# Nine places of a weight pool laid 4128 bytes apart in place of 4096, with a scratch tile of half the size

## The chip, the core and the metric

The kernel runs on one core of a Trainium2 chip. A core has a matrix engine (TensorE, PE in the profile; its loads of the stationary operand are listed apart as PEld), VectorE (DVE), ScalarE (ACT), GpSimd (POOL) and SyncE (SP, which here only issues DMAs). On-chip memory (SBUF) has 128 partitions; a place in it is a byte offset that holds for every partition alike. Matmuls read both operands from SBUF and add into PSUM. The metric is the device time of one execution in microseconds, as the median of several runs.

## The reference, cut to what matters

Two layers, each a token mixer and a SwiGLU channel mixer over 1024 positions and 1024 channels, everything in float32:

```python
D_MODEL, SEQ, DEPTH, D_FF = 1024, 1024, 2, 2816

def hybrid_mixer(h, w_in, ...):
    z = h @ w_in                                  # 1024 x 1536
    y_f = fourier_mix(z[..., :256])               # 2-D DFT over positions and 64 channels
    y_s = spatial_gating(z[..., 256:768], ...)    # gelu, layernorm, 128 x 128 position mixing
    y_a = gqa_attention(z[..., 768:1280], ...)    # 8 q heads, 2 kv heads, rotary positions
    y = jnp.concatenate([rmsnorm(y_f, ...), rmsnorm(y_s, ...), rmsnorm(y_a, ...)], axis=-1)
    return y @ w_out

def swiglu(h, w_gate, w_up, w_down):
    return (jax.nn.silu(h @ w_gate) * (h @ w_up)) @ w_down

for l in range(DEPTH):
    x = x + rmsnorm(hybrid_mixer(rmsnorm(x, g_pre_mix[l]), ...), g_post_mix[l])
    x = x + rmsnorm(swiglu(rmsnorm(x, g_pre_ffn[l]), ...), g_post_ffn[l])
```

## The kernel before

A layer goes through five stages on TensorE: the input projection (tiles `z`, `project`), attention with the DFT and the gating between its steps (`sc`, `ptr`, `pv`), the output projection (`m`, `out_steps`), the gate and up product of the channel mixer (`fx`, `fy`, `ff_prod`), and the down product (`fX`, `fY`, `d_prod`). The last two are done by a seven-product block scheme, so that DVE and POOL form sums and differences of blocks around the matmuls.

Nearly all matmuls stream 512 columns past a stationary block of 128 x 128. Float32 accuracy is had by splitting each operand into a rounded part and a remainder, both of a type called float32r (`split` and `gain_split`: ACT writes the first, DVE or POOL the second). `matmul3` (line 142) runs three matmuls for each pair: first by first, first by remainder, remainder by first. Each matmul brings its own stationary block, so TensorE loads one 128 x 128 block for each matmul, while the matmul before still streams.

The split weights live in a pool `Wp` of nine places. A tile of it holds both parts, 1024 words or 4096 bytes in each partition; the places are used in turn. In it stand the split weights of the input projection (`z_split`, line 297), nine of the sixteen of the output projection (`wo_load`, line 682), those of the gate and up product (`wsplit`, line 132, called by `ff_prep`), and half of the split operands of the down product (`d_prep`). A few others use a place for a while: an identity `id0`, a scratch row `sink`, `gpostf`, and in the last layer four rows `xin` (`ffn_open`). The order of use is that of the code; a tile waits until the readers of the tile before it at its place are done.

The other operands lie elsewhere: `nat` (all activations), the constants and `identr` (the identity of the transposes) stand before `Wp`; the raw weights `rawp` (four places of 4096 bytes), `kT`, `vv`, `hB` and others behind it, on the left side of SBUF; `hT`, `pT`, `yT`, `yFT` and others are laid from the right end down. As built, every operand of a 512-column matmul starts at 256 bytes past a multiple of 512: the large tiles on the left and those on the right all have sizes that are multiples of 512 bytes. So in 8479 of 8487 cases a streamed operand and the block that is loaded for the matmul after it start at the same offset within 512 bytes.

`junk` (line 312) is a scratch tile in which ACT leaves squares that nobody reads; only their sum is used (`sumsq`, line 152). It is 512 elements of bf16, or 1024 bytes, and stands in front of `nat` and of `Wp`.

Of the kernel before, what the change touches and what calls it, by code (L numbers as in the profile page):

```python
# [11 lines left out]
F32 = mybir.dt.float32  # L12
R32 = mybir.dt.float32r
BF16 = mybir.dt.bfloat16
# [4 lines left out]
P = 128  # L19
D = 1024  # L20
# [61 lines left out]
def encoder_kernel(ctx, tc, A, out):  # L82
# [3 lines left out]
    def pool(name, bufs=1, side="left", stack=None):  # L86
        return (stack or ctx).enter_context(tc.tile_pool(name=name, bufs=bufs, side=side, reuse_waits="tile"))

    cst = pool("cst")
    st = pool("st", 6)  # L90

    pool("edge", 1, "right").tile([P, 56], F32, name="edge")
    nat = pool("natp").tile([P, NT, D], F32, name="nat")
    Wp = pool("Wp", 9)
    rawp = pool("rawp", 4)
    psp = ctx.enter_context(tc.tile_pool(name="psp", bufs=1, space=PSUM))
# [18 lines left out]
    asp = dram.tile([DFF, S], F32, name="asp")  # L115


    def split(hi, lo, src, eng=nc.vector):
        nc.scalar.copy(hi, src)  # L119
        eng.tensor_tensor(out=lo, in0=src, in1=hi.bitcast(F32), op=ALU.subtract)  # L120

    def gain_split(w, raw, g):

        nc.scalar.activation(w[:, 0], raw, AF.Copy, scale=g)
        nc.vector.scalar_tensor_tensor(out=w[:, 1], in0=raw, scalar=g, in1=w[:, 0].bitcast(F32), op0=ALU.mult, op1=ALU.subtract)

    def fetch(src, shape, name, p=None):
        raw = (p or rawp).tile([P] + shape, F32, tag="raw", name=f"raw_{name}")
        nc.sync.dma_start(raw, src)
        return raw  # L130

    def wsplit(src, shape, name, p=None, **kw):

        w = (p or Wp).tile([P, 2] + shape, R32, tag="w", name=f"w_{name}", **kw)
        split(w[:, 0], w[:, 1], src)
        return w

    def rows2(w, r0, c0, n):

        return w[r0:r0 + 256, c0:c0 + n].rearrange("(k p) n -> p k n", p=P)  # L140
# [24 lines left out]
    def gain_row(p, src, name, **kw):  # L165
        g = p.tile([P, src.shape[-1]], F32, name=name, **kw)
        nc.sync.dma_start(g, src.partition_broadcast(P))
        return g
# [120 lines left out]
    def z_fetch(l, c, kk):  # L289
        raw = rawp.tile([P, 2, 512], F32, tag="raw", name=f"raw_z{l}_{c}_{kk}")  # L290
        o = 0
        for c0, n in CHUNK[c]:
            nc.sync.dma_start(raw[:, :, o:o + n], rows2(A["w_in"][l], kk * 256, c0, n))
            o += n
        zraw[l, c, kk] = raw

    def z_split(l, c, k):

        w = Wp.tile([P, 2, 512], R32, tag="w", name=f"w_z{l}_{c}_{k}")
        gain_split(w, zraw[l, c, k // 2][:, k % 2], gz[l][:, k:k + 1])  # L300
        zw[l, c, k] = w

# [6 lines left out]
    one, mean = scal[:, 0:1], scal[:, 1:2]  # L309
    nc.gpsimd.memset(one, 1.0)  # L310
    nc.gpsimd.memset(mean, 1.0 / 256)
    junk = cst.tile([P, 512], BF16, name="junk")
    nc.scalar.activation(junk[:, 0:8], mhalf, AF.Square)
    gz_load(0)
    z_fetch(0, 0, 0)
    id0 = Wp.tile([P, P], F32, tag="w", name="id0")
    make_identity(nc, id0)
    identr = cst.tile([P, P], R32, name="identr")
    nc.vector.tensor_copy(identr, id0)
# [6 lines left out]
        x0(t)  # L326
    rope = cst.tile([P, NT, 2, HD], F32, name="rope")
    nc.sync.dma_start(rope, A["c_rope"])
    sink = Wp.tile([P, D], F32, tag="w", name="sink")


    rz = {}
# [23 lines left out]
    for l in range(DEPTH):  # L356
# [26 lines left out]
        for i, g in enumerate(("g_q", "g_k")):  # L383
            nc.sync.dma_start(gqk[:, i, 0, :], A[g][l].partition_broadcast(P))
            a = gqk[:, i, 0, :].rearrange("p (h s f) -> p h s f", h=2, s=2)
# [296 lines left out]
        def wo_load(i):  # L682

            oc, k = i // 8, KORD[i % 8]
            if k % 2 == 0:
                wraw[oc, k // 2] = fetch(rows2(A["w_out"][l], k * P, oc * 512, 512), [2, 512], f"wo{l}_{oc}_{k}", wr if i < 10 else (y2 if i == 14 else rawp))
            raw, g = wraw[oc, k // 2][:, k % 2], gmx[:, k:k + 1]
            w = (Wp if i < 9 else (Yr if i < 11 else W2)).tile([P, 2, 512], R32, tag="w", name=f"w_wo{l}_{oc}_{k}")
            if i < 10:
                nc.gpsimd.tensor_tensor(out=raw, in0=raw, in1=g.to_broadcast([P, 512]), op=ALU.mult)  # L690
                nc.scalar.copy(w[:, 0], raw)
                nc.gpsimd.tensor_tensor(out=w[:, 1], in0=raw, in1=w[:, 0].bitcast(F32), op=ALU.subtract)
            else:
                gain_split(w, raw, g)
            wo[oc, k] = w
# [101 lines left out]
        Yr = pool(f"Yr{l}", 2, "right", sY)  # L797
# [11 lines left out]
        for n, G in enumerate(groups):  # L809
            nxt = groups[n + 1] if n + 1 < len(groups) else None  # L810
            t, g = G
# [56 lines left out]
        W2 = pool(f"W2{l}", 5, "left", sL)  # L868
        yp = pool(f"yp{l}", 1, "right", sY)
        y2 = pool(f"y2{l}", 1, "right", sR)  # L870
        gpost = gain_row(yp, A["g_post_mix"][l], f"gpost{l}")
# [157 lines left out]
        def d_unit(kind, i, shape, dt, name):  # L1029
            p = du[kind]  # L1030
            return p.tile([P] + shape, dt, tag=f"{kind}{i}", name=name, bufs=1)
# [22 lines left out]
        def d_blk(gi, pi, side, b):  # L1054

            r, c = divmod(b, 10)
            j, h = (c, r) if side == 0 else (r, c)
            return draw[gi, pi, side, j - 1][:, (h - 1) * 512:h * 512]

        def d_sums(gi, v):  # L1060
            for pi in range(len(DGROUPS[gi])):
                a = lambda b: d_blk(gi, pi, 0, b)
                w = lambda b: d_blk(gi, pi, 1, b)
                tt = lambda o, x, y, op=ALU.subtract: nc.gpsimd.tensor_tensor(out=o, in0=x, in1=y, op=op)  # L1064
                if v == 5:
                    tt(a(11), a(11), a(21))
                    tt(a(21), a(21), a(22), ALU.add)
                    tt(w(11), w(12), w(11))
                    tt(w(12), w(22), w(12))
                elif v == 6:  # L1070
                    tt(a(21), a(22), a(11))
                    tt(w(11), w(22), w(11))
                elif v == 3:
                    tt(a(12), a(12), a(21))
                elif v == 4:
                    tt(w(21), w(21), w(11))
# [3 lines left out]
        def d_op_slot(s, n):  # L1080

            gi, v = STEPS[s]
            if len(DGROUPS[gi]) == 3:
                return ("W", "W", "W", "W", "W", "W", "W", "W", "W", ("dO", 0), ("dO", 1), ("dO", 2),
                        ("dO", 3), ("dN", 0), ("dN", 1), ("dN", 2), ("dN", 3), ("dN", 4))[s % 3 * 6 + n]
            return {1: "W", 2: "W", 5: ("dO", n), 6: ("dN", n), 3: ("dR", 4 + n), 7: ("dR", n), 4: ("dN", n)}[v]

        def d_prep(s):
            if s >= len(STEPS):
                return  # L1090
            gi, v = STEPS[s]
            d_sums(gi, v)
            n = 0
            for pi in range(len(DGROUPS[gi])):
                for side in range(2):
                    slot = d_op_slot(s, n)
                    nm = f"dw{l}_{s}_{n}"
                    if slot == "W":
                        t = Wp.tile([P, 2, 512], R32, tag="w", name=nm)
                    else:  # L1100
                        t = d_unit(slot[0], slot[1], [2, 512], R32, nm)
                    split(t[:, 0], t[:, 1], d_blk(gi, pi, side, DOPER[v][side]), nc.gpsimd if gi + 1 == len(DGROUPS) and v in (3, 4) and pi else nc.vector)
                    dop[s, pi, side] = t
                    n += 1
# [76 lines left out]
        for n in range(NPROD):  # L1181
            p, j = divmod(n, 14)
# [31 lines left out]
        fin = {}  # L1214

        def ffn_open(t):
            own = last and t > 3
            xin = (Wp if own else rawp).tile([P, D], F32, tag="w" if own else "raw", name=f"xin{l}_{t}")
            fin[t] = Residual(t, t // 4, fin["gpost"], xs, out if last else xs, xin, None, f"po{l}_{t}")

        def fstep(spec):
# [30 lines left out]
        for s, (gi, v) in enumerate(STEPS):  # L1252
            end = gi + 1 == len(DGROUPS)
            for u in range(4):
                if not (end and v == 4):
                    d_tile(s, u)
                if end and v == 7:
                    d_tile(s + 1, u)
            k = DORD.index(v)
            if not end and k < 4:  # L1260
                for n in range(k * 3, min(k * 3 + 3, 4 * len(DGROUPS[gi + 1]))):
                    d_load(gi + 1, n)
            d_prep(s + 3)
            if end and v == 1:
                if not last:
                    rz_tile(l + 1)
                fin["gpost"] = Wp.tile([P, D], F32, tag="w", name=f"gpostf{l}")
                nc.sync.dma_start(fin["gpost"], A["g_post_ffn"][l].partition_broadcast(P))
                if not last:
                    gz_load(l + 1)  # L1270
                    for kk in range(4):
                        z_fetch(l + 1, 0, kk)
            if end and not last:
                if v in (2, 5):
                    for kk in range(4):
                        z_split(l + 1, 0, kk + (4 if v == 5 else 0))
# [34 lines left out]
```

## Time and profile before

| | us |
|---|---|
| median of 3 runs | 2283.14 (2282.67 to 2284.38) |
| the profiled execution | 2282.25 |
| its span, first to last instruction | 2280.5 |
| TensorE busy in the span | 2191.5 |
| VectorE busy | 1607.3 |
| ScalarE busy | 1138.5 |
| GpSimd busy | 952.2 |
| mean granted TensorE clock | 0.983 |

The profile is one execution, taken by the hardware. Its rows name the source line, the engine, the operation and the tiles (written from read), the number of such instructions, and their busy time. The end of a matmul is modelled, so how close matmuls follow one another is read from the start times in the timeline or from the length of a row of many; the duration of a single one is not its cost. Between the span and the execution's own time lie 1.75 us.

### The profile page before, as it was taken

What the parts mean: (1) busy time and instruction counts of PE and PEld (TensorE: products, weight loads), DVE (VectorE), ACT (ScalarE), POOL (GpSimd) and SP (SyncE); (2) the same over time, 40 slices, a digit from 0 to 9 for tenths busy, and PEclk for the clock granted to TensorE, in tenths of its full rate; (3) what the DMA queues carried; (4) which work ended last, traced back from release to release, by engine and by line L of the source; (5) the groups of instructions that cost most, each with busy time, mean ns of one, the idle gap of its engine ahead of it and who ended that gap; (6) DMA issues with size and microseconds to landing.
All of it is one profiled execution on the core that took longest, in us unless ns stands there. A gap on an engine that the chain in (4) does not pass through costs nothing. (4 is left out here: it accounts for less than half of the span.)

```text
span 2280.5 us, 29159 instructions
## 1 busy us (share of the span) xinstructions
PE 2191.5 (96%) x10460; PEld 1807.2 (79%) x10460; DVE 1607.3 (70%) x2457; ACT 1138.5 (50%) x2188; POOL 952.2 (42%) x797
## 2 busy tenths in 40 slices
PE   9999999999999999999899999999999999999986
PEld 7787888878888888877677788888788888877874
DVE  6868986585444447899977698965854444488998
ACT  6338996553333334434452489855533333344333
POOL 2643443243323235655637235332432323266556
PEclk9999999999999999999999999999999999999998
DMA  4110003213132316221331000042132323253212
GB/s 159 42 45 20 19 10 115 99 65 106 61 105 62 104 62 240 111 84 47 107 111 38 17 19 20 10 138 85 61 102 74 93 74 93 74 226 111 83 47 111
DMA packets 104961, 185.28 MB, mean 81 GB/s; under 512 B 12272, under 2 KB 62704, under 8 KB 104816
## 3 DMA queue, kind: packets, MB, share of 16 engines
q1 hardware_dynamic: 103376, 178.70, 23.1%
q0 software_dynamic: 1440, 4.72, 0.7%
q8 instruction: 82, 1.34, 0.2%
q14 instruction: 63, 0.52, 0.1%
HBM read 143.54 MB, written 39.85 MB: 80 GB/s over the span
## 5 line engine op out<-in xcount | busy, mean ns | idle before, releaser
L144 PE MATMUL fx<-hT,w_f 128*128 128x512 f32 x1584 | 374.9, 393 | 6.6 <-ACT nat L1006 4.5
L144 PEld LDWEIGHTS fx<-hT,w_f 128*128 128x128 f32 x1584 | 300.1, 190 | 71.2 <-ACT nat L1006 6.0
L120 DVE TENSOR_TENSOR w_f<-raw_f,w_f 128x512 fp32r<-128x512 f32 x264 | 213.9, 814 | 192.6 <-ACT w_f L119 189.5
L120 DVE TENSOR_TENSOR dw<-dr,dw 128x512 fp32r<-128x512 f32 x300 | 325.4, 1129 | 30.2 <-ACT dw L119 29.9
L144 PE MATMUL z<-w_z,hT 128*128 128x512 f32 x1152 | 286.3, 403 | 11.8 <-DVE rz L196 5.1
L119 ACT CAST dw<-dr 128x512 fp32r<-128x512 f32 x308 | 171.8, 618 | 234.5 <-POOL dr L1064 94.1
L119 ACT CAST w_f<-raw_f 128x512 fp32r<-128x512 f32 x264 | 162.2, 621 | 236.3 <-PE fy L144 196.7
L144 PEld LDWEIGHTS z<-w_z,hT 128*128 128x128 f32 x1152 | 216.6, 193 | 58.6 <-DVE rz L196 5.5
L144 PE MATMUL fX<-dw,dw 128*128 128x512 f32 x1056 | 248.5, 391 | 8.8 <-DVE nat L1123 8.5
L943 POOL TENSOR_TENSOR s<-raw_f,raw_f 128x512 f32<-128x512 f32 x44 | 58.9, 1338 | 459.5 <-DMA raw_f<-in_w_gate_dram 442.1
L144 PE MATMUL fy<-hB,w_f 128*128 128x512 f32 x1056 | 248.0, 390 | 1.9 <-DVE hB L120 1.9
L144 PEld LDWEIGHTS fX<-dw,dw 128*128 128x128 f32 x1056 | 197.1, 188 | 54.8 <-DVE nat L1123 13.9
L144 PEld LDWEIGHTS fy<-hB,w_f 128*128 128x128 f32 x1056 | 198.0, 188 | 43.6 <-DVE hB L120 2.7
L1064 POOL TENSOR_TENSOR dr<-dr,dr 128x512 f32<-128x512 f32 x132 | 220.0, 1696 | 8.6 <-DVE dw L120 8.6
L144 PE MATMUL fY<-dw,dw 128*128 128x512 f32 x792 | 198.3, 408 | 24.1 <-DVE nat L1123 19.3
L997 DVE TENSOR_TENSOR nat<-fy,nat 128x512 f32<-128x512 f32 x132 | 90.9, 690 | 172.3 <-PE fy L144 88.2
L144 PEld LDWEIGHTS fY<-dw,dw 128*128 128x128 f32 x792 | 156.3, 199 | 61.8 <-DVE nat L1123 21.0
L120 DVE TENSOR_TENSOR pT<-ptr,pT 128x512 fp32r<-128x512 f32 x256 | 171.8, 685 | 35.9 <-ACT pT L119 33.5
L752 PE MATMUL pv<-pT,vv 128*128 128x512 f32 x512 | 181.0, 434 | 0.3 <-DVE pT L120 0.3
L119 ACT CAST pT<-ptr 128x512 fp32r<-128x512 f32 x256 | 150.6, 595 | 40.4 <-PE ptr L740 38.1
L1006 ACT COPY nat<-fx 128x512 f32<-128x512 f32 x132 | 77.6, 588 | 183.4 <-PE fx L144 177.7
L723 DVE TENSOR_REDUCE mx<-sc 128x1 f32<-128x1024 f32 x128 | 155.9, 1220 | 10.9 <-PE sc L720 8.9
(208 smaller groups left out, 3746.5 us busy)
## 6 DMA issues: line engine op xcount, KB each, us to landing
raw_f<-in_w_gate_dram SPq DMA_DIRECT2D x44, 512.0 KB, 3.6
raw_f<-in_w_up_dram SPq DMA_DIRECT2D x44, 512.0 KB, 4.1
asp<-nat SPq DMA_DIRECT2D x88, 256.0 KB, 2.6
dr<-in_w_down_dram SPq DMA_DIRECT2D x44, 512.0 KB, 6.1
dr<-asp SPq DMA_DIRECT2D x44, 512.0 KB, 6.5
xin<-xs SPq DMA_DIRECT2D x24, 512.0 KB, 3.3
raw_z<-in_w_in_dram SPq DMA_DIRECT2D x16, 512.0 KB, 4.1
raw_wo<-in_w_out_dram SPq DMA_DIRECT2D x16, 512.0 KB, 3.7
```

The costliest lines, as they stand in the source:

```text
L119: nc.scalar.copy(hi, src)
L120: eng.tensor_tensor(out=lo, in0=src, in1=hi.bitcast(F32), op=ALU.subtract)
L144: nc.tensor.matmul(ps, lhs(a), rhs(b), start=first and i == 0, stop=last and i == 2, **kw)
L723: nc.vector.tensor_reduce(mx, sc, axis=AX.X, op=ALU.min)
L752: nc.tensor.matmul(pv, vv[:, kt, g].rearrange("p i d -> p (i d)"), pT[:, i], start=(kt == 0 and i == 0), stop=(kt == 7 and i == 1))
L943: tt = lambda o, x, y, op: nc.gpsimd.tensor_tensor(out=o, in0=x, in1=y, op=op)
L997: nc.vector.tensor_tensor(out=t, in0=acc, in1=t, op=ALU.add)
L1006: nc.scalar.copy(t, X)
L1064: tt = lambda o, x, y, op=ALU.subtract: nc.gpsimd.tensor_tensor(out=o, in0=x, in1=y, op=op)
```

## The change

A helper `wtile` takes every tile of `Wp` as 1024 + 8 words and hands out the first 1024 (or fewer) of them, in the shape that is asked for. So the nine places are 4128 bytes apart. `junk` becomes uint8, 512 bytes in place of 1024. Where `d_prep`, `z_split`, `wo_load`, `wsplit` and others took a tile from `Wp`, they now call `wtile`.

The instructions of every engine, their order and their waits are the same before and after; only places and the type of `junk` differ. `nat` and the constants behind `junk` move down by 512 bytes, so they keep their offset within 512. The nine places of `Wp` start at 256, 288, 320, 352, 384, 416, 448, 480 and 0 bytes past a multiple of 512. What is laid behind `Wp` on the left (raw weights, `kT`, `vv`, `hB`, operands of the down product) moves down by 512 and up by 9 x 32 = 288 bytes, and so starts at 32 past a multiple of 512. What is laid from the right stays at 256. Of the 8487 pairs of a 512-column stream and the next stationary block, 1795 still start at the same offset within 512 bytes, and the others at one of 18 other distances. 3824 of the streams start at an odd multiple of 32 bytes.

```diff
+    PAD = 8
     Wp = pool("Wp", 9)
...
+    def wtile(shape, dt, name):
+
+        t = Wp.tile([P, 1024 + PAD], dt, tag="w", name=name)
+        if len(shape) == 1:
+            return t[:, 0:shape[0]]
+        if len(shape) == 2:
+            return t[:, 0:1024].rearrange("p (a n) -> p a n", a=2)
+        return t[:, 0:1024].rearrange("p (a k n) -> p a k n", a=2, k=shape[1])
...
-        w = (p or Wp).tile([P, 2] + shape, R32, tag="w", name=f"w_{name}", **kw)
+        w = wtile([2] + shape, R32, f"w_{name}")
         split(w[:, 0], w[:, 1], src)
...
-        w = Wp.tile([P, 2, 512], R32, tag="w", name=f"w_z{l}_{c}_{k}")
+        w = wtile([2, 512], R32, f"w_z{l}_{c}_{k}")
...
-    junk = cst.tile([P, 512], BF16, name="junk")
+    junk = cst.tile([P, 512], mybir.dt.uint8, name="junk")
...
-    id0 = Wp.tile([P, P], F32, tag="w", name="id0")
+    id0 = wtile([P], F32, "id0")
...
-    sink = Wp.tile([P, D], F32, tag="w", name="sink")
+    sink = wtile([D], F32, "sink")
...
-            w = (Wp if i < 9 else (Yr if i < 11 else W2)).tile([P, 2, 512], R32, tag="w", name=f"w_wo{l}_{oc}_{k}")
+            w = wtile([2, 512], R32, f"w_wo{l}_{oc}_{k}") if i < 9 else (Yr if i < 11 else W2).tile([P, 2, 512], R32, tag="w", name=f"w_wo{l}_{oc}_{k}")
...
-                        t = Wp.tile([P, 2, 512], R32, tag="w", name=nm)
+                        t = wtile([2, 512], R32, nm)
...
-            xin = (Wp if own else rawp).tile([P, D], F32, tag="w" if own else "raw", name=f"xin{l}_{t}")
+            xin = wtile([D], F32, f"xin{l}_{t}") if own else rawp.tile([P, D], F32, tag="raw", name=f"xin{l}_{t}")
...
-                fin["gpost"] = Wp.tile([P, D], F32, tag="w", name=f"gpostf{l}")
+                fin["gpost"] = wtile([D], F32, f"gpostf{l}")
```

## The prediction, made before the changed kernel ran

> **What bounds the kernel now.** I read the page's busy times first, then the busy times by stage, then who waits on TensorE, and last the chain of waits.
>
> ```profile
> span 2280.5 us, 29159 instructions
> PE 2191.5 (96%) x10460; PEld 1807.2 (79%) x10460; DVE 1607.3 (70%) x2457; ACT 1138.5 (50%) x2188; POOL 952.2 (42%) x797
> ```
>
> ```profile
> 480.00:890.00 410.00, 405.56 (x1779) 334.67 (x1778) 216.37 (x279) 159.39 (x279) 134.32 (x93) 1.00 0.30 95
> 890.00:1110.00 220.00, 203.95 (x862) 164.85 (x861) 201.56 (x229) 94.65 (x173) 140.30 (x85) 0.96 0.26 95
> 2240.00:2280.50 40.50, 22.13 (x95) 17.12 (x93) 34.16 (x50) 15.99 (x36) 24.96 (x21) 0.84 0.25 104
> ```
>
> The second fence is busy time by stage: start and end, length, then PE, PEld, DVE, ACT, POOL, granted clock, DMA share. In the gate and up product (480 to 890) TensorE is busy 405.56 of 410 us and nobody else is near. In the down product (890 to 1110) VectorE has 201.56 of 220 us beside TensorE's 203.95. In the last 40 us VectorE leads. So the kernel is a stream of matmuls, and what one matmul costs sets the time nearly everywhere.
>
> ```profile
> PE fY L144 <- DVE nat L1123: 19.3, 6, 4.9
> PE fX L144 <- DVE nat L1123: 8.5, 8, 2.2
> PE sc L720 <- ACT pj L733: 7.4, 6, 1.8
> ```
>
> These are the three longest sums of what TensorE waits for (us, times, longest): 35 us of 2280. No wait can be worth more than its few us here; only the cost of each matmul could be. That cost I read from the chain of waits in the gate and up product, where the pieces follow without a hole:
>
> ```profile
> 1662.80 20.85 PE fx L144 x92
> 1683.65 5.44 PE fy L144 x24
> 1689.09 0.91 PE fx L144 x4
> 1690.00 10.88 PE fy L144 x48
> 1700.88 20.85 PE fx L144 x92
> ```
>
> One pair of column blocks takes 1700.88 - 1662.80 = 38.08 us for 92 + 24 + 4 + 48 = 168 matmuls: **226.7 ns each**. The kernel has 8488 matmuls of that form (the sum over its tile groups): 8488 x 226.7 ns = 1924 us, 84% of the span.
>
> **The change part by part.** No instruction, order or wait changes on any engine; what changes is where operands lie, and one output type. So there are four terms.
>
> *1. Streams and weight loads that no longer start at the same offset.* This is the only large one. What could offset cost today? A price has to come out of the 226.7 ns. Matmuls of 256 columns give the part that does not grow with columns:
>
> ```profile
> 148.74 1.60 PE L144 MATMUL vf<-dft,ut 128*128 128x256 f32 x12
> L144 PE MATMUL vf<-dft,ut 128*128 128x256 f32 x96 | 12.5, 283 | 0.0
> ```
>
> Twelve of them take 1.60 us from the first start to the last end, and the last lasts 0.283, so they follow one another at (1.60 - 0.283) / 11 = 119.7 ns. The other 256 columns of the large form cost 226.7 - 119.7 = 107.0 ns; two times that is 214.0, and 226.7 - 214.0 = **12.7 ns** is a fixed part of each matmul. A weight load is a fixed 512 bytes per partition too, so the fixed part could be the load that disturbs the stream because both start at the same offset. If it all were and all went, 8488 x 12.7 ns = 107.8 us would go: that is the lower bound. I take nothing, for three reasons in the trace. First, the load itself takes no notice of the stream:
>
> ```profile
> L144 PEld LDWEIGHTS fx<-hT,w_f 128*128 128x128 f32 x1584 | 300.1, 190 | 71.2 <-ACT nat L1006 6.0 <-DVE hT L120 2.9
> L621 PEld LDWEIGHTS ms<-scal,sq 128*128 128x128 f32 x32 | 4.5, 190 | 2.9 <-DVE sq L614 1.5 <-issue 0.5 <-PE z L144 0.5
> L740 PEld LDWEIGHTS ptr<-identr,pj 128*128 128x128 f32 x1024 | 125.8, 141 | 31.0 <-ACT pj L733 1.3 <-ACT qT L710 0.7 <-DVE pT L120 0.5
> ```
>
> It takes 190 ns (mean) in `fx`, where 512 columns stream beside it, and 190 in `ms`, where each matmul streams a single column. Second, the attention has transposes, whose load (`pj`) and stream (`identr`) also start at the same offset:
>
> ```profile
> 200.38 0.60 PE L740 MATMUL ptr<-identr,pj 128*128 128x128 f32 x4
> L740 PE MATMUL ptr<-identr,pj 128*128 128x128 f32 x1024 | 154.4, 273 | 0.8 <-ACT pj L733 0.8
> ```
>
> They follow at (0.60 - 0.273) / 3 = 109 ns for 128 columns. At 107.0 ns for 256 columns that is two passes, and about 2 ns are left. So the same meeting leaves 2 ns in one form and 12.7 in the other: the fixed part goes with the form of the matmul. Third, there are a few loads that read one word in place of 512 bytes and lie at another offset (480 to 504 bytes from the stream's start): the broadcast rows of `rb`, loaded while a score matmul streams.
>
> ```profile
> 220.13 0.63 PE L720 MATMUL sc<-kT,qT 128*128 128x512 f32 x2
> 220.36 0.65 PEld L631 LDWEIGHTS rb<-identr,rf 128*128 128x128 f32 x4
> 220.60 0.61 PE L631 MATMUL rb<-identr,rf 128*128 128x128 f32 x4
> ```
>
> The second `sc` starts at about 220.36 (its length of 0.40 before the end of the row), with the load of `rb` beside it, and `rb` follows at 220.60: 0.23 to 0.24 us, no less than the 226.7 ns beside an ordinary load. Take the meeting away, and the fixed part stays. This third row is the nearest to what the change does, so the term is **0**, with 0 to -107.8 us as its range on this side.
>
> The Trainium skill, page "TensorE: Matmul & The Clock Gate", section "Step-by-step: what each phase is for", speaks against this change: it says that TensorE reads the stream and the weights through two independent ports, so a load takes nothing from the running stream; the trace agrees with it (190 ns and 190 ns above). The same page, section "Back-to-back issue gap", gives about 216 ns for an isolated matmul of 512 columns; as an estimate from that page, a kernel that came down to it would gain 8488 x (226.7 - 216) = 91 us, and the rows above do not say that place is what stands between.
>
> *2. Streams and loads that now start at an odd multiple of 32 bytes* (3824 of the streams). Everything starts at 256 past a multiple of 512 today, so no row shows such a stream. The nearest is the load of `rb`, which starts at odd words:
>
> ```profile
> L631 PEld LDWEIGHTS rb<-identr,rf x32: 187/190/192, 220.4 to 1389.3; 128*128 128x128 f32 x32
> ```
>
> Its min, median and max are 187, 190 and 192 ns, the usual load. Bounds: nothing, or one fetched piece more for each stream. If a piece were 64 bytes, that is 16 columns at 107.0 / 256 = 0.418 ns: 6.7 ns, and 3824 x 6.7 ns = 25.6 us. I take 0, since `rb` is the nearest row.
>
> *3. DMAs into places 32 past a multiple of 512* (the raw weights and what lies behind `Wp`, four `xin` and two `gpostf` in it).
>
> ```profile
> raw_f<-in_w_gate_dram SPq DMA_DIRECT2D x44, 512.0 KB, 3.6
> xin<-xs SPq DMA_DIRECT2D x24, 512.0 KB, 3.3
> PE tp_h L174 <- DMA nat<-in_x_dram: 4.4, 1, 4.4
> 2195.95 5.63 DMA xin<-xs
> ```
>
> TensorE waits for a DMA only once, 4.4 us at the start, into `nat`, whose offset stays. In the chain of waits a DMA into a shifted place stands once, at 2195.95. Bytes in rows of 1 KB (`w_gate`) land in 3.6 us, the same bytes in rows of 4 KB (`xs`) in 3.3: four times as many pieces cost 0.3 us, so a piece more in some rows is bounded by 0 and 0.3 us there, and by as much again for the first weights at the start. The cover of the others is a stage of 410 us in which TensorE does not wait for them; without it each of 88 loads could cost up to 0.3 us, 26 us. I take 0.
>
> *4. Squares written as one byte in place of two.*
>
> ```profile
> L154 ACT ACTIVATE junk<-nat x96: 399/632/659, 153.3 to 2268.0; 128x512 bf16<-128x512 f32 x80, 128x256 bf16<-128x256 f32 x16
> L119 ACT CAST w_f<-raw_f x264: 603/622/626, 455.0 to 2002.9; 128x512 fp32r<-128x512 f32 x132
> ```
>
> The three numbers are min, median and max in ns. An ACT pass of this size takes 632 ns with a two-byte output and 622 with a four-byte one, so the width moves it by some 10 ns: 96 x 10 ns = 1 us on an engine that is half idle, of which a handful stand in the last 40 us. Bounds -0.1 to +0.1 us on the path; I take 0.
>
> *Sum.* 0 + 0 + 0 + 0 on the profiled execution's 2282.25 us (2280.5 of span and 1.75 around it). It lies 0.89 us below the median of the runs shown, so I forecast **2283.0 us**, between the two and next to the median. VectorE and GpSimd meet at other moments when anything shifts, and the stages in which they lead (the down products and the end) then move by some us: 2279 to 2288 is this case's own range.
>
> **The rivals.** *Meeting does cost, and goes (faster).* For it: 12.7 ns of each matmul are not explained by its columns, they are a fixed amount, and 8479 of 8487 pairs start at the same offset today, so the trace has hardly any other case to show. Against it: the three rows of term 1. Of the pairs, 6692 move apart. Without the 1848 of the down product, where VectorE is as long as TensorE, some 6692 x 6640 / 8488 = 5235 matmuls would each save 12.7 ns: 66.5 us, 2216 us; if only half of the distances help, 2250.
>
> *Odd starts cost (slower).* The mechanism of term 2, in the input projection, the gate and up product and the down product: a stream that starts in the middle of a fetched piece needs one more. It decides from the point at which a piece is over 32 bytes and the next is not fetched ahead. 25.6 us more: 2309 us; up to 2320 if loads pay too. Against it: the load of `rb`.
>
> *Landings cost a little (slower).* Term 3 with less cover than I think: a tenth of the 26 us shows, with some drift in the down products: 2289 to 2295. The Trainium skill, page "DMA: Bandwidth & Descriptors", section "How a descriptor splits into AXI transactions", says that a piece that does not start at a multiple of 256 bytes costs a transaction more; as an estimate from that page rows of 1 KB would need 5 in place of 4. It was at such a multiple before and is not any more; no run so far shows the other side.
>
> *The change doesn't do what it says.* 1795 of 8487 pairs still meet, and those of `sc` all do, since `kT` and `qT` move together. That gives the forecast's time, too.
>
> **How the numbers follow.** About 0.2%, or 4.6 us, is what a measurement of this kernel can tell from no change. Forecast and the empty change 0.75; meeting goes 0.09, and a gain of a few us by drift 0.03; odd starts 0.08; landings 0.05. So faster 0.12, within 0.2% 0.75, slower 0.13. The range of 8 in 10 holds the forecast's own range, the landings and half of the drift: 2275 to 2296; the large gain (0.09) and the odd starts (0.08) are left out.
>
> **What would show it.** If I am right, the chain of waits of the changed kernel has the same 38.08 us for 168 matmuls (within 0.1), and `fx` at 226.7 ns whichever place its weights have. If meeting cost, it falls towards 36 us, while `sc` keeps its time. If odd starts cost, it grows towards 39, and a row of 12 matmuls is longer at every second place of `Wp`. If landings cost, the median of `raw_f` grows by 0.3 us or more, and TensorE waits for `raw_f` or `dr`. If the squares cost, `junk` is off 632 ns. I would be wrong in term 1 if the place in SBUF, and not the form of the matmul, made the 12.7 ns: `rb` is only eight cases.

## The result and the profile after

The changed kernel takes 2306.2 us (median of 3 runs, 2305.83 to 2306.82) where the kernel before took 2283.14: 1.01 times as long, with a 95% interval of 1.0077 to 1.0123. The forecast was 2283.0 within 2275 to 2296; the measured time is 23 us above it.

The head of the page after, with busy time, share of the span and instructions of each engine:

```profile
span 2305.0 us, 29159 instructions
PE 2222.0 (96%) x10460; PEld 1803.9 (78%) x10460; DVE 1610.9 (70%) x2457; ACT 1138.8 (49%) x2188; POOL 954.1 (41%) x797
```

The span grew by 24.5 us, TensorE's busy time by 30.5, and nobody else's by more than 3.6. The chain of waits after, in the gate and up product (start, length, what, all in us):

```profile
1681.65 21.27 PE fx L154 x92
1702.92 5.60 PE fy L154 x24
1708.52 0.93 PE fx L154 x4
1709.44 11.16 PE fy L154 x48
1720.61 21.35 PE fx L154 x92
```

The same 168 matmuls take 1720.61 - 1681.65 = 38.96 us where they took 38.08: 231.9 ns each in place of 226.7. And the piece of 92 is 21.27 us once and 21.35 the next time, where it had 20.85 every time: which place of `Wp` a block of weights got now shows in the time.

The start times of successive matmuls in the trace give the whole account. Their distances, added up by stage, after less before, in us:

```
gate and up product   +19.5
input projection       +3.5
output projection      +3.3
attention and gating   +1.8
down product           -3.6
sum                   +24.6
```

The gate and up product has 3696 matmuls; 19.5 us are 5.3 ns for each. In the down product the matmuls are slower too (`fX` 231.3 ns, before 227.1, over distances below 260 ns), and yet the stage's sum fell. Two things in the trace run the other way. TensorE's waits became shorter (engine, what waited for whom, us, times, longest):

```profile
PE fY L154 <- DVE nat L1133: 15.7, 5, 4.5
PE fX L154 <- DVE nat L1133: 8.6, 7, 2.1
PE fY L154 <- ACT dw L129: 3.3, 2, 1.7
```

They were 19.3, 8.5 and 4.7, so 5 us are gone. And TensorE ran there for less time at half its clock (a granted clock of 0.5). In the first down product (start and end, length, PE, PEld, DVE, ACT, POOL, granted clock, DMA share) the clock is 0.98, where the same stretch had 0.96 before:

```profile
890.00:1110.00 220.00, 207.20 (x875) 165.62 (x873) 199.65 (x220) 94.05 (x171) 144.31 (x88) 0.98 0.28 103
```

In both down products together the stretches at half clock, in which such a matmul takes 427 ns, last 13.7 us in place of 34.1. The run with a distance of 64 below has 34.1 us of them like the kernel before, and there the down product took 1.8 us more. So the -3.6 is what is left of slower matmuls, shorter waits and more clock; why the full clock was granted for longer is not shown.

The other things that the forecast named as signs:

```profile
L154 PEld LDWEIGHTS fx<-hT,w_f 128*128 128x128 f32 x1584 | 301.6, 191 | 79.5 <-ACT nat L1016 5.8 <-DVE hT L130 3.0
raw_f<-in_w_gate_dram SPq DMA_DIRECT2D x44, 512.0 KB, 4.0
L164 ACT ACTIVATE junk<-nat x96: 400/631/659, 155.4 to 2292.5; 128x512 uint8<-128x512 f32 x80, 128x256 uint8<-128x256 f32 x16
```

A weight load still lasts 191 ns (190 before), the raw weights land in 4.0 us (3.6), and the squares take 631 ns as median (632). The 0.4 us of the raw weights meet the first half of the forecast's sign for late landings, but not its second: the only DMA that TensorE waits for is still the first one into `nat`, 4.4 us. So the loss is in the matmuls' succession alone.

What does the succession look like one by one? Before, it is 225 to 228 ns for 3600 of the 3696 matmuls of the gate and up product. It wanders behind a break, that is, behind transposes or a wait. Here are the distances in ns between the starts of successive `z` matmuls from 62.344 us on in the trace of before, right behind a group of transposes:

```
228 234 236 224 230 237 228 233 231 226 227 226 227 227 227 226 226 227
```

It wanders for nine matmuls, and then settles at 226.7. After the change it hardly ever settles. The median distances in the products of the gate and up stage, by how many bytes the stream's start lies ahead of its weights' start, modulo 256 (7th to 11th matmul of a product of 12; 31 to 50 products in each row, distances below 260 ns):

```
ahead by      after: ns of each, 7th to 11th
  0           227 226 227 226 227
 32           232 234 234 234 232
 96           232 237 231 232 237
128           230 236 230 237 231
192           236 231 236 231 236
```

At 0 it settles, some six matmuls into the product. Elsewhere it goes round in patterns such as 236, 231, 236, 231. I took this as **theory A**: a run of matmuls settles at 226.7 ns if stream and next load keep the same offset, modulo 256 bytes, and wanders between 225 and 239 ns if not. Its rivals were **B**, that a stream pays for a start at an odd multiple of 32 bytes (3824 x 6.7 ns, 25.6 us, is close to what was lost), and **C**, that the DMAs into places that are off by 32 bytes cost it.

### The profile page after: what moved, and what is told of

The parts are those of the page before. It is cut to its first block, busy times and chain, and to the rows that moved or that the text cites. A ratio compares the mean times of both kernels' runs of the same rounds, so it can differ in the third digit from the quotient of the medians.

```text
span 2305.0 us, 29159 instructions
## 1 busy us (share of the span) xinstructions
PE 2222.0 (96%) x10460; PEld 1803.9 (78%) x10460; DVE 1610.9 (70%) x2457; ACT 1138.8 (49%) x2188; POOL 954.1 (41%) x797
## 5 line engine op out<-in xcount | busy, mean ns | idle before, releaser
L154 PE MATMUL fx<-hT,w_f 128*128 128x512 f32 x1584 | 384.5, 399 | 6.6 <-ACT nat L1016 4.3
L154 PE MATMUL fy<-hB,w_f 128*128 128x512 f32 x1056 | 253.4, 395 | 1.0 <-DVE hB L130 1.0
```

Of the source, the lines that this page charges most:

```text
L154: nc.tensor.matmul(ps, lhs(a), rhs(b), start=first and i == 0, stop=last and i == 2, **kw)
```

## The experiments

All kernels compute the whole result. The first four ran beside the kernel before (2283.37 us, median of 19) on the same chip.

**1. Every operand at an odd multiple of 32 bytes, all at the same offset.** The smaller `junk` and nine places of 4096 bytes, a gap of 288 bytes ahead of `Wp`, and a larger tile at the right end:

```diff
+    pool("gap").tile([P, 72], F32, name="gap")
     Wp = pool("Wp", 9)
...
-    pool("edge", 1, "right").tile([P, 56], F32, name="edge")
+    pool("edge", 1, "right").tile([P, 112], F32, name="edge")
```

> All nine places 4096 bytes apart as before, but every operand of a 512-column matmul, left and right alike, starts at 32 bytes past a multiple of 512; stream and next load still start at the same offset. Theory A (a run of matmuls settles at 226.7 ns when stream and next load keep the same offset within 256 bytes, and wanders between 225 and 239 ns, 232 on average, when not): 2283 us, within 4, and fx at 226.7 ns. Theory B (a stream that starts at an odd multiple of 32 bytes costs some 6 ns): all 8488 matmuls pay, 2320 to 2335 us, fx at 233 ns. Theory C (DMAs into places 32 past a multiple of 512 are what costs): raw_f and dr land as late as after the change, 2290 to 2306 us with fx at 226.7 ns.

Measured: 2285.06 us, 1.0008 times before (0.9999 to 1.0018). The chain of waits of this kernel:

```profile
1665.55 20.85 PE fx L145 x92
1686.41 5.44 PE fy L145 x24
1691.85 0.91 PE fx L145 x4
1692.75 10.88 PE fy L145 x48
1703.63 20.85 PE fx L145 x92
```

38.08 us again, piece by piece as before. All streams and loads start at an odd multiple of 32, and nothing is lost that this comparison can tell. B falls, and with it the rival of the forecast that came closest in time. C falls as well: the raw weights land at 32 past a multiple of 512, as they do with the change.

**2. Left and right 64 bytes apart.** The gap ahead of `Wp` is 64 bytes, the right end as before:

```diff
+    pool("gap").tile([P, 16], F32, name="gap")
     Wp = pool("Wp", 9)
```

> Nine places 4096 bytes apart; everything from the weights' pool on, on the left side, starts at 320 past a multiple of 512, the right side stays at 256, so that 4527 pairs of stream and next load are 64 bytes apart (in one direction or the other) and the others at the same offset; no start at an odd multiple of 32. Theory A: fx and fy from the left side's hB stay at 226.7 ns, those with hT go to 230 to 234 ns; some 3300 such matmuls outside the down product by 3 to 6 ns are 10 to 20 us: 2293 to 2303 us. Theory B: no odd start, 2283 us within 4. Theory C: DMAs land at a multiple of 64, at most as late as after the change: 2283 to 2306 us with all at 226.7 ns.

Measured: 2299.33 us, 1.0075 (1.006 to 1.009). No place is padded here, and all weights start at the same offset, so in the gate and up product a stream is either at distance 0 or 64 bytes behind its weights, which is 192 ahead modulo 256. The profiled execution was the longest of four, 2304.92 us at a mean clock of 0.982 (the others 2297.96 to 2299.72 at 0.985 to 0.987); the rows below lie in a stretch at full clock. The timeline of TensorE (start, length, what) shows both kinds beside each other, since `T1`, one of the tiles named `hT`, and both of `hB` lie on the left with the weights, and the others on the right:

```profile
1710.84 5.60 PE L145 MATMUL fy<-hT,w_f 128*128 128x512 f32 x24
1716.28 5.76 PE L145 MATMUL fx<-hT,w_f 128*128 128x512 f32 x24
1737.65 5.76 PE L145 MATMUL fy<-hB,w_f 128*128 128x512 f32 x24
1744.18 5.61 PE L145 MATMUL fy<-hB,w_f 128*128 128x512 f32 x24
```

With some 0.39 us for the last matmul of a row, (5.60 - 0.39) / 23 = 226.5 ns where stream and weights share the offset (`T1`, and the second row of `hB`), and (5.76 - 0.39) / 23 = 233.5 ns where they are 64 bytes apart. (The row at 1737.65 is named `hB` too, but streams `B22`, which lies on the right.) This is the mechanism in one kernel, with the same instructions in the same order: 7 ns for each matmul whose stream is off its weights. A holds in what it says of the distance. It does not hold in the wandering: 64 apart, 1995 of 2077 distances between starts lie between 232 and 235 ns, from the first matmul of a row on.

**3. The same with 256 bytes.**

```diff
+    pool("gap").tile([P, 64], F32, name="gap")
     Wp = pool("Wp", 9)
```

> As the run with a distance of 64, but with 256 bytes between the left side and the right: 3952 pairs at the same offset within 512, 4527 pairs at 256. Theory A with a period of 256 bytes: 2283 us within 4, both fx<-hT and fx<-hB at 226.7 ns. Theory A with a period of 512: fx<-hT unsettled, 229 to 234 ns, 2290 to 2303 us. Theory B: 2283 us within 4.

Measured: 2283.64 us, 1.0001 (0.9991 to 1.001). The first piece of the 168 matmuls in the chain of waits, and the first of the next 168:

```profile
1663.96 20.85 PE fx L145 x92
1702.04 20.85 PE fx L145 x92
```

38.08 us. 256 bytes count as none. The run says two things more. `junk` is one byte wide here and `nat` 512 bytes lower, as in the change, so neither costs anything. And the median landing of `raw_f` from `w_gate` was 3.8 us at a start of 0 modulo 512, 3.9 in the first two runs and in the next, 3.6 and 4.0 before and after: it does not go with the offset.

**4. The change, with all behind `Wp` put back.** Only the nine places are spread:

```diff
     Wp = pool("Wp", 9)
+    pool("gap").tile([P, 56], F32, name="gap")
     rawp = pool("rawp", 4)
```

> The change, with 224 bytes left empty behind the weights' pool, so that the raw weights, kT, vv, hB and all else behind it start at 256 past a multiple of 512 again; only the nine places are spread. Theory A: 5656 pairs differ (6692 with the change), so most of the loss stays: 2297 to 2306 us, fx and fy at about 232 ns. Theory B: 1008 streams start at an odd multiple of 32 (3824 with the change): 2287 to 2292 us, and only input and output projection are longer. Theory C: the raw weights land where they did before, 2283 us within 4.

Measured: 2302.17 us, 1.0085 (1.0068 to 1.0102), which is 19 of the 23 us. The same two pieces of its chain of waits:

```profile
1675.37 21.23 PE fx L155 x92
1714.21 21.41 PE fx L155 x92
```

38.84 us: nearly the change's 38.96. The spread of the nine places is the cause, and their knock-on on what lies behind them the rest. The share goes with the pairs that differ, 5656 in place of 6692, more than with odd starts, 1008 in place of 3824.

**5 and 6. Small distances.** Is there one that beats 0? The weights stay, and the streamed tiles of the gate and up product get room for 64 words more, in which each is moved by a number of words of its own (single runs, the kernel before beside them 2285.26 us):

```diff
+        OFF = {'B11': 1, 'B21': 2, 'T2': 3, 'T3': 4, 'T4': 6, 'B22': 8}
+
+        def placed(p, nm, vs):
+            t = p.tile([P, 4096 * len(vs) + 64], R32, name=nm)
+            return {v: t[:, 4096 * i + OFF[v]:4096 * (i + 1) + OFF[v]].rearrange("p (a k n) -> p a k n", a=2, k=4) for i, v in enumerate(vs)}
+
+        hv = placed(hp, f"hB_{l}", ("B11", "B21"))
-        hv = {v: hp.tile([P, 2, 4, 512], R32, name=f"h{v}_{l}") for v in ("B11", "B21")}
```

> Places 4096 bytes apart as before; of the seven streamed operands of the gate and up product one (T1) keeps the offset of the weights, and six start 4, 8, 12, 16, 24 and 32 bytes further within 256. Theory A1 (only a multiple of 256 settles): the products of all six take 229 to 234 ns a matmul, T1's 227 to 228; 3168 matmuls by 3 to 6 ns: 2292 to 2302 us. Theory A2 (places are told apart in pieces of 16 or 32 bytes): those within the piece settle at 226.7 ns like the distance 0, and the first that leaves it does not; 2286 to 2296 us. Theory A3 (some small distance is better than none): at least one of the six settles below 226 ns.

In the second, `OFF` is 12, 62, 16, 48, 56 and 60 words:

> The same with streams 48 bytes ahead of the weights (B11), 8 behind (B21), 64 ahead (T2), 64 behind (T3), 32 behind (T4) and 16 behind (B22), within 256. Theory A1: all between 229 and 234 ns. Theory A2: 8 (and 16) behind settle at 226.7 ns, the rest as in the change: 64 ahead 229.6, 64 behind 233, 32 behind 233. Theory A3: one of them below 226 ns.

Measured: 2306.33 us and 2296.1 us. By the distances between starts in these two traces and in that of the change:

```
stream ahead of weights by (bytes, modulo 256)
    0     4     8    12    16    24    32    48    64    96   128   160   192   224   240   248
mean ns of a matmul in the gate and up product
227.3 236.8 232.5 229.2 232.0 234.7 233.2 232.9 229.6 233.4 232.7 233.8 233.1 233.1 228.4 232.2
   e5    e5    e5    e5    e5    e5    e5    e6    e6 after after after    e6    e6    e6    e6
```

(e5 and e6 are the two runs; the 227.3 at 0 includes the first matmuls of each product, which come from another distance.) None is below 0, so A3 falls and I found no version that beats the kernel before. A2 falls, too: 4 bytes off is the worst of all, and 8 behind (248) has a mean of 232.2 and does not settle. Of A1 the direction holds but neither its band nor its rule: 4 bytes cost 10 ns, and so the first run came out above the 2292 to 2302 I had given, and 16 bytes behind (240) does settle. There the first matmul of a product takes 233 ns and all behind it 227, as medians, and the mean of 228.4 comes from the starts. Added up, the six of the first run are (10.1 + 5.8 + 2.5 + 5.3 + 8.0 + 6.5) ns x 528 = 20.2 us over 226.7; 21 us were measured. Those of the second run are 15.4 us, and 10.8 were measured; with one execution of each kernel, nothing can be read from that difference.

## Why the prediction was wrong

*What bounds the kernel* was right: the cost of each matmul sets the time, and this is where it changed.

*Term 1 failed, in its sign.* It asked what the meeting at one offset costs, gave it 0 to -107.8 us, and left out that the meeting may be what keeps the matmuls at their pace. It had 12.7 ns of each matmul as the price of a collision that might be relieved. No run relieved them: in none of the seven kernels did the gate and up product settle below 226.7 ns at any distance, and moving apart costs 2 to 10 ns more on average. So what the term had at 0 is 5.3 ns for each matmul of that product, on the other side. The likeliest value, 0, was taken from `rb`, and that row was misread: 0.23 to 0.24 us for a score matmul beside a load that lies elsewhere was set down as "no less than 226.7", but the profile's other rows had settled matmuls at 226.7, and 0.235 is what an unsettled one takes (the eight of them lie between 226 and 236 ns). Score matmuls stand four in a row between transposes and never settle; they are at 231.7 ns on average before and 231.8 after. The succession behind a break, 228, 234, 236, 224, stood in the trace of before and would have shown that the pace of a matmul depends on something that is not in its form.

*The reasons under term 1* were right in what they say of the load: it lasts 190 ns with and without a stream, and still does. What they could not say is what the stream suffers, since the trace has no true end of a matmul. So the Trainium skill's sentence that a load takes nothing from the running stream (page "TensorE: Matmul & The Clock Gate", section "Step-by-step: what each phase is for") agreed with the row on the load. It does not agree with the second run, where 64 bytes between the two cost 7 ns of each matmul, nor with the ends of the products (below).

*Term 2 and the rival of the odd starts.* The rival's 2309 us is near the 2306 measured, and its mechanism is refuted: the first run has all starts odd and loses nothing. Its 25.6 us were the wrong reason for nearly the right number; the gate and up product's 3696 matmuls by 5.3 ns, with some us from the projections, are the right one. The forecast's sign for the rival, a chain that grows towards 39 us, came true as well (38.96) and could not tell the two apart. *Terms 3 and 4* were right: no DMA wait of TensorE but the one at the start, and no time from the squares.

*The stage that was left out.* The rival of the meeting left the down product out, since VectorE is as long there. The outcome was as it assumed, since the matmuls got slower there and the stage did not, but in part by luck: the change's trace also had 20 us less at half clock in that stage.

*The load or the own weights.* Within a product a stream has the same distance from its own weights as from the load for the next matmul. Where one product ends and the next begins, the two differ, and there the traces of the change and of the fourth run tell them apart. These are the last matmuls of their products whose own weights are at distance 0 and which follow four settled ones (224 to 228 ns), by how far their stream starts ahead of the next load, modulo 256:

```
ahead of the next load        0     64     96    128    192    224
mean ns to the next start  226.6  225.8    236  232.5  225.9  235.0
how many                     16     32      2      4     22     19
```

All have the same distance to their own weights, and yet their time goes with the load. The next product's own distance does not explain it either: in the change's trace five of these matmuls take 234 to 235 ns with a load at 224 where the next product is at 0 again, and four take 226 to 227 with a load at 0 where it is at 32. So it is the place of the load beside the running stream that counts.

*What stays open.* The runs show that the distance counts modulo 256 bytes and which distances settle, but not what in the chip does it. One load at 64 or 192 costs nothing yet, while rows at 192 take 233 ns for each matmul: how the cost builds up over successive loads was not tested. How far the change of distance from product to product adds to the distance itself was not measured alone either; the second run, with 233.5 ns along rows of 24 that stay 64 apart, shows that the distance is enough.

## What to carry to other kernels

Where float32r matmuls of 512 columns with a new stationary block each follow without a hole, keep the starts of streamed and stationary operands equal modulo 256 bytes, across pools and on both sides of SBUF, and look at a pad of a few words as at a change of the matmul's pace. A regular pattern that everything shares may be what holds the pace, so give such a term a bound on both sides, even if the trace only shows one. And read the matmuls' pace from start to start, right behind a break as well as in the steady run: a pace that varies there says that something beyond the columns is at work.

## What the runs showed of the hardware that I had not expected

A run of matmuls has a state. Behind the break shown above it wanders between 224 and 237 ns for nine matmuls and then settles at 226.7, with equal offsets. Coming from another distance, it needs some six matmuls to settle. With the change, most distances go round in a pattern of their own (236, 231, 236, 231 at 192 ahead), but in the second run the same 192 gave a steady 233.3; why is open. A single word of distance counts: 4 bytes cost 10 ns, 12 bytes 2.5. And matmuls of 256 columns went the other way; the twelve of `vf` are a little faster with the change, where their stream starts 32 bytes ahead of its weights modulo 256 (1.56 us, 1.60 before):

```profile
150.86 1.56 PE L154 MATMUL vf<-dft,ut 128*128 128x256 f32 x12
```

That is (1.56 - 0.28) / 11 = 116.4 ns for each in place of 119.7, with too few of them (96) to show in the total.
